# First value sums of a two-layer encoder: x transposed, cast and squared in a different order

## The chip, the cores and the metric

The kernel runs on one core of a Trainium2 chip. A core has five engines that run side by side and wait for each other through semaphores: TensorE (PE, matrix products, into PSUM), VectorE (DVE), ScalarE (ACT), GpSimd (POOL) and SyncE (SP, which here only issues DMA transfers). Each engine works through its instructions in the order in which they were issued. The metric is the device time of one execution in microseconds (us), lower is better.

## The reference

The reference is an encoder of two layers over 256 tokens of 1024 values, in float32. Each layer has a token mixer (RMSNorm, one wide input projection `w_in`, a pooling mixer, dilated attention, gates, an output projection) and a gated MLP with a short convolution. Only the very beginning of layer 0 matters here:

```python
def _rmsnorm(x, g):
    xf = x.astype(jnp.float32)
    y = xf * lax.rsqrt(jnp.mean(xf * xf, axis=-1, keepdims=True) + EPS)
    return (y * g.astype(jnp.float32)).astype(x.dtype)
...
u, q, k, v, g_pool, g_attn = jnp.split(xn @ w_in, SPLITS, axis=-1)   # xn = _rmsnorm(x, norm1)
```

## The kernel before

**Products in two parts.** TensorE multiplies in a rounded format (float32r). To keep float32's precision, every operand is split into a rounded part and a rest: h = round(a), l = a - h. A product of two such operands is three products: h*h, l*h, h*l. ScalarE makes the rounded parts ("casts") and VectorE the rests. For weights the parts are the tiles `wh` and `wl`; for x they are `xuh` and `xul`.

**Weights.** The class `Weights` (line 95) holds the list of all weight loads and of the pieces into which each load is cut. A load is 1 MB, issued by SP into one of three buffers `raw`; the next load into a buffer is issued once VectorE has made the last rest of the old one. A piece is cast into one of five pairs of buffers `wh`, `wl` (`BUFS = 5`); the buffers of piece n come free for piece n + 5 when TensorE has done its last product with piece n. The first four pieces (loads 0 and 1) and load 2 lie in tiles of their own that are needed for something else later. In layer 0, the first twelve pieces (two chunks of 128 rows by 512 columns each) belong to the values v, four to each of three groups: pieces 0 to 3 to group 0, 4 to 7 (loads 2 and 3) to group 1, 8 to 11 (loads 4 and 5) to group 2. These are multiplied by the norm's gain on the way (lines 195 to 206), one chunk of 128 x 512 per instruction. Piece 12 is the first one of the pooling projection and is cast as a whole, 128 x 1024 (line 191).

**The start of layer 0.** The mean square of x is not known when the first products could start. So `begin_values_of_x` (line 600) multiplies x as it is by the scaled weights of group 0, and the row factor (`rs`, 1 over the root of the mean square) is put on the sums afterwards (`keep_values`, line 769). x comes in four transfers: two token halves (t = 0, 1) by two halves of the 1024 values. TensorE turns x chunk by chunk of 128 values (`turn_x`, line 613, 16 transposes `xt_ps` in all), ScalarE casts the turned chunks to `xuh`, VectorE makes the rests `xul`. `square` (line 626) gives the sum of squares of one half of the values of one token half: on ScalarE for the first half of the values (line 630), on VectorE for the second (line 634); GpSimd adds them up and takes the power (lines 639 to 642). `whole` (line 644) adds `xuh` and `xul` back to a float32 x in turned form, four chunks at once (128 x 1024), for the normed x that the other projections need. `both(k)` is the cast and the rest of weight chunk k, `products` issues the products of (token half, chunk, kinds). All this is inside a hand-written order (line 785): each engine gets these instructions exactly as they are written.

**What follows.** `first_values` (line 724) transposes the two row factors (`r_ps`, line 732), scales the float32 x by gain and row factor on VectorE (line 736, eight instructions), casts it (`x2`, line 741, ScalarE, four) and takes the rests (line 742, VectorE, four). In between it keeps the sums of group 0 and computes groups 1 and 2 with 96 products on TensorE (line 754): group 1 needs pieces 4 to 7, group 2 pieces 8 to 11. Then come the parameters (`load_params`, line 355: small loads, two transposes at line 364) and the pooling projections (`proj`, line 497, products at line 492), which use `x2` and piece 12 onward. From `first_values` on, the order on each engine is not written by hand: a scheduler orders the instructions by its own estimates of when each could run. The rest of both layers is a long stream of such projections.

**Names used below.** A chunk is 128 rows of weights, or 128 values of x. A weight's rest is `wl`, and a row such as "L200 DVE wl" makes one.

Of the kernel before, what the change touches and what calls it, by code (L numbers as in the profile page):

```python
# [10 lines left out]
F32 = mybir.dt.float32  # L11
F32R = mybir.dt.float32r
AF = mybir.ActivationFunctionType
ALU = mybir.AluOpType
AX = mybir.AxisListType

P = 128
D = 1024
S = 256
DEPTH = 2  # L20
KD = D // P
# [199 lines left out]
def encoder(ctx, tc, x, w_in, w_pool, pool_scale, w_a, w_b, w_o, norm1, norm2, w_up, conv_w,  # L221
            conv_b, w_down, rel_bias, norm_f, onehot, edges, out):
    nc = tc.nc
# [5 lines left out]
    mmp = ctx.enter_context(tc.tile_pool(name="mmp", bufs=4, space=bass.MemoryType.PSUM))  # L229
# [21 lines left out]
    for l in range(DEPTH):  # L251
        for g in range(NG):
            c0 = C_V + g * 512
            slots = (("m2", 0, 2), ("m2", 1, 2), ("ybig",), ("at2",)) if g == 0 else ()
            for j in range(2):
                tag = "k1" if l == 0 and g == 1 and j == 0 else None
# [44 lines left out]
    h = const.tile([P, 2, D], F32, name="h")  # L301
# [7 lines left out]
    ident = const.tile([P, P], F32, name="ident")  # L309
# [4 lines left out]
    def begin():  # L314


        rows8 = sm.tile([KD, P], F32, tag="gain", bufs=1, name="grows")
        nc.scalar.dma_start(out=rows8, in_=norm1[0].rearrange("(k p) -> k p", p=P))
        first, second = W.load_by(4), W.load_by(2)

        def part_of_x(t, n):
            nc.sync.dma_start(out=h[:, t, HALVES[n]], in_=xv[:, t, HALVES[n]])

        part_of_x(0, 0)
        next(first)
        part_of_x(1, 0)
        for _ in range(3):
            next(first)
        part_of_x(0, 1)
        part_of_x(1, 1)  # L330
        for _ in range(2):
            next(second)
        W.load(4)
        ones = sm.tile([P, P], F32, tag="s", name="ones")
        nc.vector.memset(ones, 1.0)
        make_identity(nc, ident)
        nc.vector.memset(mhalf, -0.5)
        ps = mmp.tile([P, P], F32, tag="mm", name="gain_ps")
        warm(ps, ones, WARM[0])
        nc.tensor.transpose(ps[:, 0:KD], rows8, ident[:KD, :KD])  # L340
        nc.vector.tensor_copy(gcol, ps[:, 0:KD])
        ps = mmp.tile([P, P], F32, tag="mm", name="warm_ps")
        warm(ps, ones, WARM[1])
        return lambda n: warm(ps, ones, n)
# [255 lines left out]
    def begin_values_of_x():  # L600


        more = begin()
        W.gains = gcol

        raw_x = [
            big.tile([P, KD, 2, P], F32R, tag=tag, name=name) for tag, name in (("xn", "xuh"), ("q1", "xul"))
        ]
        xuh, xul = raw_x
        ss = [sm.tile([P, 4], F32, tag="ss", name="ss") for _ in range(2)]  # L610
        rs = [sm.tile([P, 1], F32, tag="rstd", name="rstd") for _ in range(2)]

        def turn_x(t, c0, n=4):

            ks = slice(c0, c0 + n)
            pt = mmp.tile([P, n, P], F32, tag="mm", name="xt_ps")
            for k in range(n):
                nc.tensor.transpose(pt[:, k, :], h[:, t, (c0 + k) * P : (c0 + k + 1) * P], ident)  # L618

            def keep():  # L620
                nc.scalar.copy(out=xuh[:, ks, t, :], in_=pt)
                nc.vector.tensor_sub(out=xul[:, ks, t, :], in0=pt, in1=xuh[:, ks, t, :].bitcast(F32))

            return keep

        def square(t, n):
            cc = HALVES[n]
            junk = sm.tile([P, 512], F32, tag="p", bufs=3, name="junk")
            if n == 0:
                nc.scalar.activation(  # L630
                    junk, h[:, t, cc], AF.Square, scale=D**-0.5, accum_out=ss[t][:, n : n + 1]
                )
            else:
                nc.vector.scalar_tensor_tensor(
                    out=junk, in0=h[:, t, cc], scalar=1.0 / D, in1=h[:, t, cc],
                    op0=ALU.mult, op1=ALU.mult, accum_out=ss[t][:, n : n + 1],
                )
            if n == 0:
                nc.gpsimd.tensor_scalar_add(ss[t][:, 3:4], ss[t][:, 0:1], EPS)
            else:  # L640
                nc.gpsimd.tensor_add(out=ss[t][:, 3:4], in0=ss[t][:, 3:4], in1=ss[t][:, 1:2])
                return nc.gpsimd.tensor_tensor(out=rs[t], in0=ss[t][:, 3:4], in1=mhalf, op=ALU.pow)

        def whole(n, tag):

            ks = slice(4 * n, 4 * n + 4)
            f = big.tile([P, 4, 2, P], F32, tag=tag, name="xu")
            nc.vector.tensor_add(out=f, in0=xuh[:, ks].bitcast(F32), in1=xul[:, ks].bitcast(F32))
            return f

        ps = [v_tile() for _ in range(2)]
        chunks, pieces = {}, []

        def split(k):
            if k % 2 == 0:
                pieces.append(W.n_split)
                chunks[k], chunks[k + 1] = W.open_next()
            return chunks[k]

        def product(t, k, kind):  # L660
            wh, wl = W.split[pieces[k // 2]]
            a, w = {"hh": (xuh, wh), "lh": (xul, wh), "hl": (xuh, wl)}[kind]
            first = k == 0 and kind == "hh"
            last = k == KD - 1 and kind == ("lh" if t else "hl")
            return nc.tensor.matmul(ps[t], a[:, k, t, :], w[:, k % 2, :], start=first, stop=last)  # L665

        def both(k):

            hi, lo, _ = split(k)
            hi()  # L670
            return lo()

        def products(*steps):
            for t, k, kinds in steps:
                for kind in kinds:
                    last = product(t, k, kind)
            return last

        keep = turn_x(0, 0, 2), turn_x(0, 2, 2)
        more(WARM[2])  # L680
        _, lo, hi = split(0)
        hi()
        keep[0]()
        products((0, 0, ("hh",)))
        keep = keep[1], turn_x(1, 0)
        lo()
        products((0, 0, ("lh", "hl")))
        keep[0]()
        keep[1]()
        both(1)  # L690
        products((1, 0, ("hh", "hl", "lh")))
        products(*((t, 1, (kind,)) for kind in ("hh", "lh", "hl") for t in range(2)))
        both(2)
        products(*((t, 2, ("hh", "lh", "hl")) for t in range(2)))
        keep = turn_x(0, 4)
        both(3)
        square(0, 0)
        square(1, 0)
        square(0, 1)
        f0 = whole(0, "q0")  # L700
        keep()
        products((0, 3, ("hh", "lh", "hl")))
        keep = turn_x(1, 4)
        both(4)
        keep()
        W.load(5)
        products((1, 3, ("hh", "lh", "hl")), (0, 4, ("hh", "lh", "hl")))
        both(5)
        pool = square(1, 1)
        products((1, 4, ("hh", "lh", "hl")), (0, 5, ("hh", "lh", "hl")))  # L710
        for k in range(6, KD):
            both(k)
            products((1, k - 1, ("hh", "lh", "hl")), (0, k, ("hh", "lh", "hl")))
        f1 = whole(1, "k0")
        pe = products((1, KD - 1, ("hh", "hl", "lh")))
        W.load(6)
        W.n_got = W.n_split
        for _ in range(4):
            for hi, lo, *_ in W.open_next():
                act, dve = hi(), lo()  # L720
        W.queue_behind((act, dve, pool), 4)
        return rs, raw_x, (f0, f1), ps, pe

    def first_values(rs, raw_x, fs, done, pe, keep_values):

# [36 lines left out]
    for l in range(DEPTH):  # L762
# [25 lines left out]
        else:  # L788
            for g in range(NG):
                held = begun[0] if g == 0 else [W.get() for _ in range(4)]  # L790
                for t in range(2):
                    if g + t == 0:
                        ps = begun[1]
                    else:
                        ps = v_tile()
# [18 lines left out]
        for gi in range(3, -1, -1):  # L814
# [10 lines left out]
            cur, n = u, S + 2 * PAD  # L825
            sh = 1
            while sh < w:
# [3 lines left out]
                    out=nxt[:, :, 0:n], in0=cur[:, :, 0:n], in1=cur[:, :, sh : sh + n]  # L831
# [7 lines left out]
            if hw > 1:  # L839
# [5 lines left out]
                out=pd, in0=cur[:, :, o : o + S], scalar=1.0 / w, in1=u[:, :, PAD : PAD + S],  # L845
                op0=ALU.mult, op1=ALU.subtract,
            )
            both = pl2[gi // 2][:, gi % 2 * 2 : gi % 2 * 2 + 2]
# [115 lines left out]
        for m, c in enumerate(PAIRS):  # L964
# [7 lines left out]
            for n in range(4):  # L972
# [4 lines left out]
                scale = HD**-0.5 if n < 2 else 1.0  # L977
                if hd < HPG:
# [3 lines left out]
                        out=lo[:, hd], in0=src, scalar=scale, in1=hi[:, hd].bitcast(F32),  # L982
                        op0=ALU.mult, op1=ALU.subtract,
                    )
                    nc.vector.scalar_tensor_tensor(
                        out=lo[:, hd], in0=rest, scalar=scale, in1=lo[:, hd].bitcast(F32),
                        op0=ALU.mult, op1=ALU.add,
                    )
                else:
# [3 lines left out]
                        out=o, in0=src, scalar=scale, in1=o, op0=ALU.mult, op1=ALU.add  # L993
# [20 lines left out]
        for c in range(KD):  # L1014
            th = gate(c)
            nc.vector.scalar_tensor_tensor(
                out=pa[:, c, :], in0=th, scalar=1.0, in1=pa[:, c, :], op0=ALU.add, op1=ALU.mult
# [3 lines left out]
        for c4 in range(2):  # L1021
            ths = [gate(4 * c4 + j) for j in range(4)]
            for j2 in range(2):
                i, (wh, wl) = W.get()
                for j in range(2):
                    c = 4 * c4 + 2 * j2 + j
                    ps = mmp.tile([P, 2, S], F32, tag="mm", name="b_ps")
                    cc = slice(j * P, (j + 1) * P)
# [4 lines left out]
                        out=m, in0=ths[2 * j2 + j], scalar=1.0, in1=m, op0=ALU.add, op1=ALU.mult  # L1033
# [49 lines left out]
        held, ps = entry  # L1083
        first = keep_entry(ps)
        ps = v_tile()
# [106 lines left out]
```

## Time and profile before

| what | value |
|---|---|
| median of 3 runs | 876.4 us (876.33 to 876.72) |
| the profiled execution's own time | 876.65 us |
| its span, first to last instruction | 874.9 us |
| TensorE busy | 867.3 us, 99% of the span |
| VectorE busy | 683.2 us, 78% |
| ScalarE busy | 523.2 us, 60% |
| GpSimd busy | 32.3 us, 4% |
| mean granted TensorE clock | 0.997 |
| read from memory | 159.8 MB, 184 GB/s over the span |

"Busy" is the time in which an engine had an instruction in work. TensorE's products overlap, so a row of it is longer than the distance to the next row. In a timeline a row gives the start and the length in us, the engine, the line, the operation, what it writes and reads, the shape, and how many equal instructions are put together; in brackets stands how long the engine had been idle before and what it waited for. Line numbers of the profile are those of the kernel before; in the changed kernel, lines behind the edited functions are higher by 5 or 6.

### The profile page before, as it was taken

To read this page: it belongs to the slowest core of one execution; us is meant where nothing else is said; L and a number is where in the kernel's file an instruction comes from. 1 tells how busy PE (TensorE), PEld (TensorE's weight loads), DVE (VectorE), ACT (ScalarE), POOL (GpSimd) and SP (SyncE) were. 2 spreads that over 40 slices of the span, in tenths; PEclk is the share of its full clock that TensorE was granted. 3 is DMA by queue.
4 is the path that set the end of the run, shared out by engine and by line. 5 is a ranking of instruction groups with operands and counts; after the bars stand their busy time and mean duration, and the time that the engine had idled before them with its cause. 6 is when DMAs were issued, how large, how long until landed. Compare 5 with 4: busy or idle time off the path is not lost.

```text
span 874.9 us, 12732 instructions
## 1 busy us (share of the span) xinstructions
PE 867.3 (99%) x4803; PEld 756.2 (86%) x4803; DVE 683.2 (78%) x1160; ACT 523.2 (60%) x927; POOL 32.3 (4%) x98
## 2 busy tenths in 40 slices
PE   9999999999999999999999999999999999999997
PEld 7888898988888888888888888898888888888886
DVE  7998786767869988878756988676678698877874
ACT  6756554556747766666545564554666486656662
POOL 2700000000000000000000000000000000000000
PEclk9999999999999999999999999999999999999998
DMA  9675645355555465465737465543556447456441
GB/s 331 228 250 198 199 153 171 124 172 190 177 186 194 163 226 189 167 219 191 241 121 240 145 215 171 163 161 121 186 189 216 152 150 254 164 193 210 175 145 49
DMA packets 125958, 161.70 MB, mean 185 GB/s; under 512 B 3320, under 2 KB 106432, under 8 KB 125896
## 3 DMA queue, kind: packets, MB, share of 16 engines
q1 hardware_dynamic: 125880, 160.88, 54.5%
q8 instruction: 38, 0.62, 0.3%
q14 instruction: 24, 0.20, 0.1%
q10 hardware_dynamic: 16, 0.00, 0.0%
HBM read 159.80 MB, written 1.07 MB: 184 GB/s over the span
## 4 chain that ended last, share of the span: by engine, by line
PE 99%; ACT 0%; POOLq 0%; DVE 0%; issue 0%; POOL 0%; ACTq 0%
PE proj_ps L492 61%; PE v_ps L590 6%; PE res_ps L520 6%; PE res_ps L522 6%; PE res_ps L521 6%; PE b_ps L492 3%; PE v_ps L754 2%; PE v_ps L665 1%; PE pool_ps L492 1%; PE o_ps L945 1%; PE s_ps L895 1%; PE pt_ps L924 1%; PE s_ps L890 1%; PE o_ps L941 1%; PE xt_ps L458 1%; PE xt_ps L618 0%
## 5 line engine op out<-in xcount | busy, mean ns | idle before, releaser
L192 DVE TENSOR_TENSOR wl<-raw,wh 128x1024 fp32r<-128x1024 f32 x274 | 333.9, 1223 | 85.1 <-ACT wh L191 83.3
L492 PE MATMUL proj_ps<-x,wh 128*128 128x512 f32 x1408 | 343.7, 392 | 0.0
L191 ACT CAST wh<-raw 128x1024 fp32r<-128x1024 f32 x274 | 286.8, 1050 | 78.9 <-PE res_ps L522 39.0
L492 PEld LDWEIGHTS proj_ps<-x,wh 128*128 128x128 f32 x1408 | 257.7, 188 | 49.3
L492 PEld LDWEIGHTS proj_ps<-x,wl 128*128 128x128 f32 x1408 | 180.8, 191 | 6.9
L492 PE MATMUL proj_ps<-x,wl 128*128 128x256 f32 x1408 | 183.7, 283 | 0.0
L520 PE MATMUL res_ps<-wh,actq 128*128 128x512 f32 (+1 forms) x184 | 70.0, 380 | 0.0
L521 PE MATMUL res_ps<-wl,actq 128*128 128x512 f32 (+1 forms) x184 | 69.9, 380 | 0.0
L522 PE MATMUL res_ps<-wh,actk 128*128 128x512 f32 (+1 forms) x184 | 69.9, 380 | 0.0
L1105 ACT ACTIVATE y<-a,prm 128x256 f32<-128x256 f32 x36 | 21.6, 601 | 40.5 <-DVE a L516 40.5
L521 PEld LDWEIGHTS res_ps<-wl,actq 128*128 128x128 f32 x184 | 34.6, 188 | 6.6
L520 PEld LDWEIGHTS res_ps<-wh,actq 128*128 128x128 f32 x184 | 34.6, 188 | 6.6
L522 PEld LDWEIGHTS res_ps<-wh,actk 128*128 128x128 f32 x184 | 34.6, 188 | 6.6
L492 PE MATMUL proj_ps<-po,wh 128*128 128x512 f32 x128 | 32.2, 396 | 0.0
L431 POOL TENSOR_SCALAR ss<-ss 128x1 f32<-128x1 f32 x8 | 2.1, 266 | 800.3 <-ACT junk L424 800.3
L1106 DVE SCALAR_TENSOR_TENSOR y<-a,prm,y 128x255 f32<-128x255 f32 x36 | 17.3, 482 | 14.1 <-ACT y L1105 14.1
L492 PEld LDWEIGHTS proj_ps<-po,wh 128*128 128x128 f32 x128 | 23.1, 189 | 4.2
L424 ACT ACTIVATE junk<-h 128x512 f32<-128x512 f32 (+1 forms) x20 | 11.0, 548 | 26.4 <-DVE h L422 26.4
L520 PE MATMUL res_ps<-wh,m 128*128 128x512 f32 (+1 forms) x72 | 26.5, 368 | 0.0
L522 PE MATMUL res_ps<-wh,m 128*128 128x512 f32 (+1 forms) x72 | 26.3, 366 | 0.0
L521 PE MATMUL res_ps<-wl,m 128*128 128x512 f32 (+1 forms) x72 | 26.3, 365 | 0.0
L590 PE MATMUL v_ps<-wh,x 128*128 128x512 f32 x80 | 25.7, 392 | 0.0
(202 smaller groups left out, 1125.5 us busy)
## 6 DMA issues: line engine op xcount, KB each, us to landing
raw<-in_w_in_dram SPq DMA_DIRECT2D x58, 1024.0 KB, 5.9
raw<-in_w_up_dram SPq DMA_DIRECT2D x44, 1024.0 KB, 5.1
raw<-in_w_down_dram SPq DMA_DIRECT2D x22, 1024.0 KB, 4.9
raw<-in_w_a_dram SPq DMA_DIRECT2D x8, 1024.0 KB, 5.0
raw<-in_w_o_dram SPq DMA_DIRECT2D x8, 1024.0 KB, 4.9
raw<-in_w_b_dram SPq DMA_DIRECT2D x4, 1024.0 KB, 4.8
raw<-in_w_pool_dram SPq DMA_DIRECT2D x2, 1024.0 KB, 5.1
gain<-in_norm_dram SPq DMA_DIRECT2D x3, 512.0 KB, 4.6
```

Source lines behind the costliest of these rows:

```text
L191: lambda: nc.scalar.copy(out=h, in_=src),
L192: lambda: nc.vector.tensor_sub(out=l, in0=src, in1=h.bitcast(F32)),
L424: nc.scalar.activation(junk[:, 0 : cc.stop - cc.start], h[:, t, cc], AF.Square, scale=D**-0.5, accum_out=ss[:, n : n + 1],)
L458: nc.tensor.transpose(pt[:, k, :], xn[:, c0 : c0 + P], ident)
L492: nc.tensor.matmul(out, w(k), x, start=(n == 0), stop=(n == 2 * nk - 1), skip_group_check=turns["rest"])
L520: nc.tensor.matmul(ps, ah, wh, start=first, stop=False)
L521: nc.tensor.matmul(ps, ah, wl, start=False, stop=False)
L522: nc.tensor.matmul(ps, al, wh, start=False, stop=last)
L590: nc.tensor.matmul(ps, x2[:, 2 * n + j, part, t, :], w[:, j, :], start=(n + m == 0), stop=(n == 3 and m == 5),)
L754: nc.tensor.matmul(ps[t], a[:, k, t, :], w[:, j, :], start=(k + m == 0), stop=(k == KD - 1 and m == 2),)
L1105: nc.scalar.activation(y, a, AF.Identity, bias=b, scale=w1)
L1106: nc.vector.scalar_tensor_tensor(out=y[:, 1:], in0=a[:, : S - 1], scalar=w0, in1=y[:, 1:], op0=ALU.mult, op1=ALU.add)
```

## The change

Nothing is computed differently; the transfers and the number of transposes, casts of weights and products stay as they are. In `begin_values_of_x`:

- `turn_x` takes a list of token halves. At the start it turns, casts and rests chunks 0 and 1 of token half 0, then chunks 0 and 1 of token half 1, then chunks 2 and 3 of both token halves in one piece. Before, these were chunks 0 and 1 and chunks 2 and 3 of token half 0, and all four chunks of token half 1. Chunks 4 to 7 stay in two pieces, one for each token half; the first of them now stands among the products of chunk 2 instead of behind them.
- All four squares are done by ScalarE, and they are spread: one ahead of the cast of weight chunk 4, one ahead of chunk 5, one ahead of chunk 6, one behind chunk 7.
- The two sums `whole` are made behind the rests of pieces 5 and 7 of the weights, instead of among the rests of x and behind the rest of weight chunk 7.
- The products of chunks 0 to 2 are interleaved in another order.

```diff
--- before.py
+++ after.py
@@ -610,31 +610,32 @@
         ss = [sm.tile([P, 4], F32, tag="ss", name="ss") for _ in range(2)]
         rs = [sm.tile([P, 1], F32, tag="rstd", name="rstd") for _ in range(2)]
 
-        def turn_x(t, c0, n=4):
+        def turn_x(ts, c0, n):
+
 
             ks = slice(c0, c0 + n)
-            pt = mmp.tile([P, n, P], F32, tag="mm", name="xt_ps")
-            for k in range(n):
-                nc.tensor.transpose(pt[:, k, :], h[:, t, (c0 + k) * P : (c0 + k + 1) * P], ident)
+            pt = mmp.tile([P, n, len(ts), P], F32, tag="mm", name="xt_ps")
+            for j, t in enumerate(ts):
+                for k in range(n):
+                    nc.tensor.transpose(
+                        pt[:, k, j, :], h[:, t, (c0 + k) * P : (c0 + k + 1) * P], ident
+                    )
+            tt = slice(ts[0], ts[-1] + 1)
 
             def keep():
-                nc.scalar.copy(out=xuh[:, ks, t, :], in_=pt)
-                nc.vector.tensor_sub(out=xul[:, ks, t, :], in0=pt, in1=xuh[:, ks, t, :].bitcast(F32))
+                nc.scalar.copy(out=xuh[:, ks, tt, :], in_=pt)
+                nc.vector.tensor_sub(
+                    out=xul[:, ks, tt, :], in0=pt, in1=xuh[:, ks, tt, :].bitcast(F32)
+                )
 
             return keep
 
         def square(t, n):
             cc = HALVES[n]
             junk = sm.tile([P, 512], F32, tag="p", bufs=3, name="junk")
-            if n == 0:
-                nc.scalar.activation(
-                    junk, h[:, t, cc], AF.Square, scale=D**-0.5, accum_out=ss[t][:, n : n + 1]
-                )
-            else:
-                nc.vector.scalar_tensor_tensor(
-                    out=junk, in0=h[:, t, cc], scalar=1.0 / D, in1=h[:, t, cc],
-                    op0=ALU.mult, op1=ALU.mult, accum_out=ss[t][:, n : n + 1],
-                )
+            nc.scalar.activation(
+                junk, h[:, t, cc], AF.Square, scale=D**-0.5, accum_out=ss[t][:, n : n + 1]
+            )
             if n == 0:
                 nc.gpsimd.tensor_scalar_add(ss[t][:, 3:4], ss[t][:, 0:1], EPS)
             else:
@@ -676,50 +677,55 @@
                     last = product(t, k, kind)
             return last
 
-        keep = turn_x(0, 0, 2), turn_x(0, 2, 2)
+        every = ("hh", "lh", "hl")
+        keep = turn_x((0,), 0, 2)
         more(WARM[2])
         _, lo, hi = split(0)
         hi()
-        keep[0]()
+        keep()
         products((0, 0, ("hh",)))
-        keep = keep[1], turn_x(1, 0)
+        keep = turn_x((1,), 0, 2)
         lo()
-        products((0, 0, ("lh", "hl")))
-        keep[0]()
-        keep[1]()
+        products((0, 0, ("lh",)))
+        keep()
+        keep = turn_x((0, 1), 2, 2)
         both(1)
-        products((1, 0, ("hh", "hl", "lh")))
-        products(*((t, 1, (kind,)) for kind in ("hh", "lh", "hl") for t in range(2)))
+        products((0, 0, ("hl",)), (1, 0, ("hh", "hl", "lh")))
+        keep()
         both(2)
-        products(*((t, 2, ("hh", "lh", "hl")) for t in range(2)))
-        keep = turn_x(0, 4)
+        products((0, 1, ("hh", "lh")), (1, 1, ("hh", "lh")), (0, 1, ("hl",)), (1, 1, ("hl",)))
         both(3)
+        products((0, 2, ("hh", "lh")), (1, 2, ("hh", "lh")))
+        keep = turn_x((0,), 4, 4)
+        products((0, 2, ("hl",)), (1, 2, ("hl",)))
+        keep()
         square(0, 0)
-        square(1, 0)
-        square(0, 1)
-        f0 = whole(0, "q0")
-        keep()
-        products((0, 3, ("hh", "lh", "hl")))
-        keep = turn_x(1, 4)
+        products((0, 3, every))
+        keep = turn_x((1,), 4, 4)
         both(4)
         keep()
         W.load(5)
-        products((1, 3, ("hh", "lh", "hl")), (0, 4, ("hh", "lh", "hl")))
+        products((1, 3, every), (0, 4, every))
+        square(1, 0)
         both(5)
+        products((1, 4, every), (0, 5, every))
+        square(0, 1)
+        both(6)
+        products((1, 5, every), (0, 6, every))
+        both(7)
         pool = square(1, 1)
-        products((1, 4, ("hh", "lh", "hl")), (0, 5, ("hh", "lh", "hl")))
-        for k in range(6, KD):
-            both(k)
-            products((1, k - 1, ("hh", "lh", "hl")), (0, k, ("hh", "lh", "hl")))
-        f1 = whole(1, "k0")
+        products((1, 6, every), (0, 7, every))
         pe = products((1, KD - 1, ("hh", "hl", "lh")))
         W.load(6)
         W.n_got = W.n_split
-        for _ in range(4):
+        fs = []
+        for n in range(4):
             for hi, lo, *_ in W.open_next():
                 act, dve = hi(), lo()
+            if n % 2:
+                fs.append(whole(n // 2, ("q0", "k0")[n // 2]))
         W.queue_behind((act, dve, pool), 4)
-        return rs, raw_x, (f0, f1), ps, pe
+        return rs, raw_x, fs, ps, pe
 
     def first_values(rs, raw_x, fs, done, pe, keep_values):
```

The scheduler's order of what follows changes with it, up to about the second product of the pooling projections. On ScalarE the casts of `x2` stand further back: before, two of the four are ahead of the first cast of piece 9, and now all four are behind it. On TensorE the two transposes of the parameters and the first two products of the pooling projection (with piece 12) are now among the products of group 2: the transposes behind its first product, the pair behind the first product with piece 9. On SP the load of pieces 10 and 11 is issued behind one more of the small parameter loads. Everything later is in the same order as before.

## The prediction

> **What bounds the kernel now.** I read the page first, then the chain of waits, then the timelines of TensorE, ScalarE and VectorE, engine by engine, over the first 46 us, which is all that the change touches: set side by side, the two programs issue the same instructions in the same order on every engine from about 46 us on.
>
> ```profile
> span 874.9 us, 12732 instructions
> PE 867.3 (99%) x4803; PEld 756.2 (86%) x4803; DVE 683.2 (78%) x1160; ACT 523.2 (60%) x927; POOL 32.3 (4%) x98
> PE 99%; ACT 0%; POOLq 0%; DVE 0%; issue 0%; POOL 0%; ACTq 0%
> ```
>
> TensorE is busy for 99% of the span and is 99% of the chain. A change in the first 46 us therefore costs what it adds to TensorE's waits there, and gains what it takes from them; the dense stream behind passes it on to the end. The TensorE rows of the start (start, length, engine, line, operation, out<-in, form, count, idle time before):
>
> ```profile
> 4.26 1.06 PE L618 MATMUL xt_ps<-ident,h 128*128 128x128 f32 x4
> 7.08 0.40 PE L665 MATMUL v_ps<-m,xuh 128*128 128x512 f32 x1
> 7.69 0.74 PE L665 MATMUL v_ps<-m,xuh 128*128 128x512 f32 x2 [0.21 <-ACT xuh L621]
> 8.41 0.50 PE L665 MATMUL v_ps<-m,xul 128*128 128x512 f32 x1
> 11.51 0.60 PE L618 MATMUL xt_ps<-ident,h 128*128 128x128 f32 x4
> 14.25 0.68 PE L665 MATMUL v_ps<-ybig,xuh 128*128 128x512 f32 x2
> 14.80 0.50 PE L665 MATMUL v_ps<-ybig,xul 128*128 128x512 f32 x1
> 19.47 0.38 PE L732 MATMUL r_ps<-ident,rstd 128*128 128x128 f32 x2
> 30.58 0.39 PE L754 MATMUL v_ps<-wh,xuh 128*128 128x512 f32 x1
> ```
>
> In a dense stretch a 512-column product starts 0.227 us after the last one (its row, 0.39 long, holds 0.165 of drain), a transpose 0.109. From 7.08 to 19.47 lie 46 products and 8 transposes, 11.3 us dense, in 12.4: 1.05 us are waits (0.37 before 7.69, 0.16 before 8.41, under 0.1 before 14.25 and 14.80, and each time some 0.11 until the stream runs again). Behind 19.47 there is none: the 96 products of L754 follow each other without a gap up to 41.5. ScalarE, start and second stage:
>
> ```profile
> 8.91 1.37 ACT L199 ACTIVATE m<-raw,gcol 128x512 fp32r<-128x512 f32 x2 [0.66 <-DMA raw<-in_w_in_dram]
> 10.19 0.62 ACT L630 ACTIVATE junk<-h 128x512 f32<-128x512 f32 x1
> 10.71 0.19 ACT L630 ACTIVATION_READ_ACCUMULATOR junk<-h 128x1 f32 x1
> 26.76 1.34 ACT L199 ACTIVATE wh<-raw,gcol 128x512 fp32r<-128x512 f32 x2 [0.22 <-PE v_ps L754]
> 28.00 0.60 ACT L741 CAST x<-xu 128x512 fp32r<-128x512 f32 x1
> 28.51 0.72 ACT L199 ACTIVATE wh<-raw,gcol 128x512 fp32r<-128x512 f32 x1
> 29.14 0.60 ACT L741 CAST x<-xu 128x512 fp32r<-128x512 f32 x1
> 29.64 1.95 ACT L199 ACTIVATE wh<-raw,gcol 128x512 fp32r<-128x512 f32 x3
> 31.50 1.04 ACT L191 CAST wh<-raw 128x1024 fp32r<-128x1024 f32 x1
> ```
>
> Chunk 2 of the first weights starts at 8.91, when it lands. From 26.76 on ScalarE has no idle time up to the wide cast of piece 12, and 26.76 itself is TensorE giving back the buffer of piece 4. VectorE:
>
> ```profile
> 17.26 1.22 DVE L648 TENSOR_TENSOR xu<-xuh,xul 128x1024 f32<-128x1024 f32 x1
> 18.39 5.38 DVE L200 SCALAR_TENSOR_TENSOR wl<-raw,gcol,wh 128x512 fp32r<-128x512 f32 x8
> 29.26 0.74 DVE L200 SCALAR_TENSOR_TENSOR wl<-raw,gcol,wh 128x512 fp32r<-128x512 f32 x1
> 30.52 0.74 DVE L200 SCALAR_TENSOR_TENSOR wl<-raw,gcol,wh 128x512 fp32r<-128x512 f32 x1
> ```
>
> The two rests of piece 8 are ready at 30.00 and 31.26; TensorE wants them at 30.81 and 31.49, so VectorE is only 0.8 and 0.2 us ahead.
>
> **The change, part by part.** Pitches (start to next start) from these rows and their neighbours: scaled cast 0.62 to 0.64, square with its readout 0.62, cast of x to two parts (L741) 0.51, cast of 512 values of x 0.48, weight rest 0.66, sum of x's parts 1.14, scaling (L736) 0.39, subtraction (L742) 0.61. A result is seen by another engine some 0.05 later.
>
> *Up to the first sums.* Transposes, casts and rests come in smaller pieces, so the wait before 7.69 goes: token half 1 is cast at 6.4 instead of 7.05, chunk 1's cast follows when it lands, near 7.08 instead of 7.53, and TensorE gets through chunks 0 and 1 by 9.5. What is late next is chunk 2: landed at 8.91, cast at 9.64, first product at 9.70, a wait of 0.2 plus 0.11. From there 36 products and 8 transposes remain, 36 x 0.227 + 8 x 0.109 = 9.05, which would end at 18.86. But ScalarE now does all four squares (2 x 0.62 more), each between two casts: x's second half is cast at 11.36 (its transposes now stand behind four products of chunk 2), square to 12.46, chunk 4's cast ready at 13.19, its rest at 13.97, wanted at 13.87; the rest of x's token half 1 and chunk 5's rest come 0.05 and 0.1 late in the same way. With 0.11 each that is 0.6: 19.5 against 19.47. I take nothing. The ends: with no late rest 18.86, a gain of 0.6; with every late rest twice as late and the next square in front of it, a loss of 0.5. VectorE's two squares (0.68 each) are gone, but it only waits for ScalarE instead. GpSimd's sums (0.6 and 0.95 after a square) follow the last square, now near 16.7 to 17.4, and are done at 19.1 against 19.5 wanted: 0.4 of cover, each tenth beyond it would cost a tenth.
>
> *The sums of x's parts behind pieces 5 and 7.* ScalarE reaches piece 4 at 17.34 instead of 16.02, VectorE starts its rests at 18.1 instead of 18.39. Four rests and the first sum: 18.1 + 4 x 0.66 + 1.14 = 21.9, piece 6's first rest ready at 22.64, wanted at 22.9: 0.26 of cover, and no cost. Four more rests and the second sum: VectorE is free at 25.7, where it was at 23.69: two microseconds later in a stretch in which it was 0.2 to 0.8 us ahead.
>
> *What the order does with it.* The part of the program behind the hand-written order is put in order by a scheduler, and there three things move. ScalarE now has the first half of piece 9 ahead of all four casts of x to parts (L741), which before had two of them done by then; that half still waits for TensorE to give back piece 4's buffer, at 26.76. TensorE has two products of the first pooling projection (L492, piece 12) and the two parameter transposes (L364) moved forward among the L754 products; the pair stands behind the first product of piece 9. Nothing behind the pair can start before the wide cast of piece 12. On ScalarE that cast now has six scaled casts and four casts of x in front, counted from 26.76: 6 x 0.62 + 4 x 0.51 + 1.04 = 6.80, ready at 33.56, seen at 33.6. (The same sum with two casts of x gives 32.54 for before, which is what the row says: 31.50 + 1.04.) TensorE would come to the pair 7 products and two transposes (0.17, L364) after 30.58, at 32.34. It waits 1.26, and 0.11 to run again: 1.37. The release at 26.76 is itself a TensorE time, so an earlier or later start moves both.
>
> VectorE's lateness shows at the same place. Five scalings to 27.7, the first cast of x ready at 28.0 behind piece 9, two subtractions, three scalings: piece 8's first rest is ready at 31.2 (wanted 30.98), the second, behind another subtraction, at 32.45 (wanted about 32.0). These waits lie ahead of the pair and inside its wait; alone, if ScalarE were in time, they would cost 0.2 + 0.45 + 0.22 = 0.87. The rests of pieces 9 to 11, 1.8 us later than before, meet a TensorE that is 1.4 later plus 0.45 of moved products: 0.5 of cover, as before.
>
> *Queues.* On SP the load of piece 10's weights goes behind one small parameter load and waits for load 3's landing (18.55) instead of load 2's: issued near 18.6, not 17.36. Loads in front of it are still landing at 21.46, and its cast is due near 29; at the 5.9 us that such loads take it lands by 24.5. The next loads are given free by VectorE 1.8 us later, some 6 us ahead of use. Nothing is taken for either; if a load were late, up to 1.3.
>
> *Sum.* 0.0 + 1.37 on a profiled execution of 876.65 (span 874.9, 1.75 around it): 878.0. That execution is 0.25 above the median of 876.4; against the median, **877.8**.
>
> **Rivals.** *Waits that add up* (slower by more than 0.2%, which is 1.75 us and about what a measurement of this kernel can tell from no change): the start loses its 0.5 because the squares stand ahead of casts that TensorE wants, or rests of pieces 6 and 7 use up their 0.26; either moves the release of piece 4's buffer and the pair's wait comes on top. 876.4 + 1.37 + 0.4 to 0.9: 878.2 to 878.7, taken at 878.4. For it: ScalarE is busy without a break from 11.4 on. Against: half of the sum's small waits are under a tenth.
>
> *A late clock* (slower): four transposes take 1.06 at 4.26 and 0.60 at 11.51, pitches of 0.213 and 0.109, and the first product at the full pace is that of 7.08. So TensorE runs at half pace until about 6.9, some 5.8 us after its first instruction at 1.04. The changed order leaves it idle for 0.2 near 5.1, where it had none: two transposes and one idle multiplication are over before x is cast. If that gap starts the count anew, full pace comes at 11.1: 4.2 us at half pace lose 2.1, of which the wait for chunk 2 hides 0.3, so 1.8 on top of 1.37: 879.6. Against: before had gaps of 0.2 and more at 7.5 and the pace stayed. The Trainium skill (TensorE: Matmul & The Clock Gate, Part 1, the HAM clock gate) says that the array runs at half rate until a free-running window of some 3.4 us has been busy, and drops back only after an idle window. By that rule a spoilt window would cost one window more, an estimate of 1.3 instead of 1.8, and a gap of 0.2 would most likely spoil none; the trace agrees in the two paces.
>
> *The start gains* (slower by less): no late rest, TensorE at 19.47 0.6 earlier, the pair's wait unchanged since its start moves too, up to the 0.26 of cover on piece 6's rests: 876.4 + 1.37 - 0.3 to 0.6, 877.2.
>
> *The pair does not wait* (not slower): ScalarE is in time for piece 12, so only the start counts: 876.4 - 0.6 to 876.4, say 876.0. It needs 1.26 off the 6.80 of ScalarE's queue, which the rows of before do not give, or VectorE's waits ahead of the pair to vanish as well; otherwise their 0.87 stays.
>
> **How the numbers follow.** Forecast, 876.9 to 878.1 around 877.8: 0.46. Waits that add up, 878.4: 0.33. Late clock, 879.6: 0.07. The start gains, 877.2: 0.08. The pair does not wait, 876.0: 0.06. Range 876.7 to 879.0: it leaves out the late clock and the last case, 0.13. Slower by over 0.2% (above 878.15) is the second case, the late clock and a tail of 0.03 of the forecast: 0.43; faster (below 874.65) needs the last case and over a microsecond more, 0.02; the rest, 0.55, within.
>
> **What would show it.** In the changed kernel's timeline: the wait of 0.21 at 7.69 gone and one of 0.2 near 9.7 in its place; r_ps near 19.5; L648 among the weight rests near 20.8 and 24.6; TensorE idle before wl of piece 8 (0.2 to 0.5, released by VectorE) and before proj_ps near 33.6 (released by ScalarE, L191); everything behind 46 us later by 1.4. If r_ps comes before 19.0 or after 19.9, the start was mis-sized; if the pair starts without a wait near 32.4, the main term is wrong.

## The result, and the profile after

The changed kernel takes 879.0 us (median of 7 runs, 878.16 to 879.83), the kernel before beside it 876.4 us (876.03 to 876.72): 1.0027 times as long, with a 95% interval of 1.0017 to 1.0037. It is slower, by 0.27% or some 2.4 to 2.6 us, where the prediction had 1.4. The profiled execution takes 879.0 us, 2.35 more than that of before (876.65). Its page says of the whole:

```profile
span 877.1 us, 12735 instructions
PE 869.3 (99%) x4803; PEld 757.0 (86%) x4803; DVE 682.3 (78%) x1156; ACT 524.2 (60%) x931; POOL 30.1 (3%) x98
```

TensorE is still busy for 99% of a span that is 2.3 us longer. The instructions are as foretold: two squares, of two instructions each, less on VectorE (1156 for 1160) and more on ScalarE (931 for 927). In the changed file the lines behind the start are shifted: transposes are L620, casts of x L626, rests of x L627, squares L636, products of the start L666, sums of x's parts L649, r_ps L738, group 2's products L760, their casts and rests of x L747 and L748, and values' rests L785.

Two points split the span: the first r_ps, which ends the start, and the first product with wl of the pooling projection, which ends the stage of group 2. All the rest lasts 831.4 in every kernel of this study.

| | r_ps at | from there to the pooling projection | rest | span |
|---|---|---|---|---|
| before | 19.47 | 24.05 | 831.35 | 874.87 |
| changed | 20.39 | 25.38 | 831.36 | 877.13 |
| difference | +0.92 | +1.33 | 0.0 | +2.26 |

The stage behind r_ps has grown by nearly what the prediction's main term said, 1.37. The start, which was to cost nothing, has grown by 0.9. First the stage, in TensorE's timeline of the changed kernel (start, length, engine, line, operation, out<-in, form, count, idle time before and who ended it):

```profile
31.74 0.33 PE L364 MATMUL prm_ps<-ident,prow 96*128 96x96 f32 x2
32.08 0.50 PE L760 MATMUL v_ps<-wl,xuh 128*128 128x512 f32 x1
...
32.66 0.40 PE L760 MATMUL v_ps<-wh,xuh 128*128 128x512 f32 x1
33.34 0.51 PE L760 MATMUL v_ps<-wl,xuh 128*128 128x512 f32 x1 [0.29 <-DVE wl L200]
...
33.92 0.40 PE L760 MATMUL v_ps<-wh,xuh 128*128 128x512 f32 x1
34.49 0.74 PE L492 MATMUL proj_ps<-x,wh 128*128 128x512 f32 x2 [0.17 <-ACT wh L191]
35.07 0.40 PE L760 MATMUL v_ps<-wh,xuh 128*128 128x512 f32 x1
```

The idle time in brackets counts only what is left when a row's drain is over, so the loss is read from the starts. Between 31.74 and 32.08 lie 0.34, where the two transposes at their pitch of 0.085 need 0.17: 0.17 for the first rest of piece 8. Between 32.66 and 33.34 lie 0.68 where 0.23 would do: 0.45 for the second rest of piece 8. Between 33.92 and 34.49 lie 0.57: 0.34 for the wide cast of piece 12. Each time the next start comes 0.11 late as well, which makes 1.29 of the 1.33. The same stage on ScalarE and on VectorE:

```profile
27.62 0.73 ACT L199 ACTIVATE wh<-raw,gcol 128x512 fp32r<-128x512 f32 x1 [0.44 <-PE v_ps L760]
...
33.40 1.03 ACT L191 CAST wh<-raw 128x1024 fp32r<-128x1024 f32 x1
```

```profile
21.55 1.22 DVE L649 TENSOR_TENSOR xu<-xuh,xul 128x1024 f32<-128x1024 f32 x1
22.69 2.74 DVE L200 SCALAR_TENSOR_TENSOR wl<-raw,gcol,wh 128x512 fp32r<-128x512 f32 x4
25.34 1.22 DVE L649 TENSOR_TENSOR xu<-xuh,xul 128x1024 f32<-128x1024 f32 x1
...
31.28 0.75 DVE L200 SCALAR_TENSOR_TENSOR wl<-raw,gcol,wh 128x512 fp32r<-128x512 f32 x1
...
32.54 0.75 DVE L200 SCALAR_TENSOR_TENSOR wl<-raw,gcol,wh 128x512 fp32r<-128x512 f32 x1
...
33.80 1.41 DVE L785 SCALAR_TENSOR_TENSOR vl<-v_ps,rstd,vh 128x512 fp32r<-128x512 f32 x2
```

From TensorE's release at 27.62 to the end of the wide cast at 34.43 ScalarE has no break: 6.81, against the 6.80 that were worked out. The sums stand behind four weight rests each, at 21.55 and 25.34, later than foretold by no more than r_ps is. Now the start on TensorE:

```profile
4.69 0.63 PE L349 MATMUL warm_ps<-ones 128*128 128x128 f32 x2
5.36 0.80 PE L666 MATMUL v_ps<-m,xuh 128*128 128x512 f32 x1
...
8.94 0.57 PE L666 MATMUL v_ps<-m,xul 128*128 128x512 f32 x1
9.35 0.39 PE L666 MATMUL v_ps<-m,xuh 128*128 128x512 f32 x1
...
20.39 0.38 PE L738 MATMUL r_ps<-ident,rstd 128*128 128x128 f32 x2
```

A product of 512 columns has a row of 0.6 to 0.8 at half pace and of 0.39 at full pace. The change between them, which the granted clock in the trace puts at 9.32, came at 6.87 in the kernel before. TensorE has nothing to do from 5.12 (4.69 and two pitches of 0.213) to 5.36: this is the gap near 5.1 that the prediction's late clock spoke of. The wait before 7.69 is gone, but it is gone inside a stretch at half pace.

### The profile page after: what moved, and what is told of

It is laid out like the page before. It is cut to its first block, busy times and chain, and to the rows that moved or that the text cites. A ratio compares the mean times of both kernels' runs of the same rounds, so it can differ in the third digit from the quotient of the medians.

```text
span 877.1 us, 12735 instructions
## 1 busy us (share of the span) xinstructions
PE 869.3 (99%) x4803; PEld 757.0 (86%) x4803; DVE 682.3 (78%) x1156; ACT 524.2 (60%) x931; POOL 30.1 (3%) x98
## 4 chain that ended last, share of the span: by engine, by line
PE 95%; ACT 0%; POOLq 0%; DVE 0%; issue 0%; POOL 0%; ACTq 0%
PE proj_ps L492 61%; PE v_ps L590 6%; PE res_ps L522 6%; PE res_ps L521 6%; PE res_ps L520 6%; PE b_ps L492 3%; PE pool_ps L492 1%; PE v_ps L760 1%; PE o_ps L951 1%; PE s_ps L901 1%; PE pt_ps L930 1%; PE s_ps L896 1%; PE o_ps L947 1%; PE xt_ps L458 1%; PE a_turn L1085 0%; ACT xn L475 0%
## 5 line engine op out<-in xcount | busy, mean ns | idle before, releaser
L1112 DVE SCALAR_TENSOR_TENSOR y<-a,prm,y 128x255 f32<-128x255 f32 x36 | 17.5, 485 | 14.1 <-ACT y L1111 14.1
```

What stands on the lines that cost most here:

```text
L1112: nc.vector.scalar_tensor_tensor(out=y[:, 1:], in0=a[:, : S - 1], scalar=w0, in1=y[:, 1:], op0=ALU.mult, op1=ALU.add)
```

## The experiments

Two questions were open. Is the stage's loss due to the two moved sums, and what in it holds TensorE? And is the start late through the gap near 5.1 (below called theory gap), through a pace that comes when it likes (theory phase), or through the squares on ScalarE (theory S)? The experiments ran on three chips, each with the kernel before beside them: its median was 876.13 us beside the first four experiments, 876.21 beside the next four and 876.63 beside the last. Each ratio is against these executions; it is not the quotient of the two medians.

**The sums, put back.** The changed kernel, with both sums where they were:

```diff
+        f0 = whole(0, "q0")
         products((0, 3, every))
...
+        f1 = whole(1, "k0")
         pe = products((1, KD - 1, ("hh", "hl", "lh")))
...
-        fs = []
+        fs = [f0, f1]
...
-            if n % 2:
-                fs.append(whole(n // 2, ("q0", "k0")[n // 2]))
```

> The changed kernel with the two sums of x's parts back where they stood before. Theory P (of the +2.6 us some 1.4 are the pair's wait, which the moved sums cause through the scheduler's order, and the rest is the clock: TensorE reaches its full pace at a time that differs from one execution to the next, and the new start is exposed to it where the old one waited anyway): in this program the pair is back behind the products of group 2 and two casts of x are ahead of piece 9, so the pair's wait is gone; 876.5 to 877.8 us, median near 877.3, with r_ps near 19.5 when full pace comes at 6.9 and near 20.4 when it comes at 9.3. Theory S (the four squares on ScalarE make everything behind late, and the sums matter little): 878.5 us or more.

Measured: 877.1 us (876.13 to 879.1), ratio 1.0008 (0.9998 to 1.0018). From r_ps to the pooling projection 24.07, as before (24.05): the stage's loss is gone, with all its waits. r_ps, however, comes at 21.04, later still; full pace came at 10.07, and the first sum now stands ahead of a rest that TensorE wants:

```profile
15.77 0.73 PE L666 MATMUL v_ps<-ybig,xuh 128*128 128x512 f32 x2 [0.43 <-DVE ybig L200]
...
21.04 0.38 PE L738 MATMUL r_ps<-ident,rstd 128*128 128x128 f32 x2
```

**The sums alone.** The kernel before, with only the two sums moved as in the change:

```diff
-        f0 = whole(0, "q0")
...
-        f1 = whole(1, "k0")
...
-        for _ in range(4):
+        fs = []
+        for n in range(4):
             for hi, lo, *_ in W.open_next():
                 act, dve = hi(), lo()
+            if n % 2:
+                fs.append(whole(n // 2, ("q0", "k0")[n // 2]))
```

> The kernel before with nothing changed but the two sums of x's parts, which are made behind the rests of pieces 5 and 7. In this program's order one product of the pooling projection stands ahead of group 2's end. Theory P: the wait on ScalarE's wide cast appears, 0.9 to 1.4 us on 876.4, so 877.3 to 877.8, r_ps still near 19.5. Theory S: 876.4 to 876.8, since the squares are not moved.

Measured: 877.47 us (876.76 to 879.2), ratio 1.001 (1.0001 to 1.0019). The stage takes 24.90, 0.85 more than before, and the start 19.01. TensorE's timeline:

```profile
30.35 0.33 PE L364 MATMUL prm_ps<-ident,prow 96*128 96x96 f32 x2
30.73 0.50 PE L755 MATMUL v_ps<-wl,xuh 128*128 128x512 f32 x1
...
31.30 0.39 PE L755 MATMUL v_ps<-wh,xuh 128*128 128x512 f32 x1
31.99 0.50 PE L755 MATMUL v_ps<-wl,xuh 128*128 128x512 f32 x1 [0.30 <-DVE wl L200]
...
32.79 0.40 PE L492 MATMUL proj_ps<-x,wh 128*128 128x512 f32 x1
```

Only the two rests of piece 8 hold TensorE here: 0.2 ahead of 30.73 and 0.46 ahead of 31.99, each with 0.11 behind it, which is the stage's 0.85. The time is the one expected, but not by the expected wait on the wide cast. The scheduler brings one product of piece 12 forward, not two, and it doesn't wait. So the sums alone make the greater part of the loss, through VectorE; the wait for the wide cast is the rest of it, and it needs the other changes of the order.

**The pair, held back.** The changed kernel, with the first two products of the pooling projection not to be issued before the last product of group 2:

```diff
+                            W.last_v = nc.tensor.matmul(
...
+                with ExitStack() as held:
+                    if l == 0 and (gi, j) == (3, 0):
+                        held.enter_context(tc.issue_after(W.last_v.ins))
+                    sums = proj(x2)
-                add_up(in_order(u[:, j, PAD : PAD + S]), [halves(a) for a in proj(x2)])
+                add_up(in_order(u[:, j, PAD : PAD + S]), [halves(a) for a in sums])
```

> The changed kernel with the first products of the pooling projection held on TensorE behind the last product of group 2; nothing else is moved. The pair then can't wait for piece 12's cast. If the pair's place alone were the cost, 1.4 us less than the changed kernel, 877.6. If VectorE's late rests of piece 8 take over, as the prediction has it (0.87 of its 1.37 stays), 0.5 less: 878.5.

Measured: 879.25 us (877.67 to 879.55, 6 runs), ratio 1.0027 (1.0015 to 1.0038). That is above both of the expected figures, with full pace at 9.59. The stage takes 25.47, no less than the changed kernel's 25.38. TensorE, and VectorE at the same time:

```profile
33.51 0.50 PE L760 MATMUL v_ps<-wl,xuh 128*128 128x512 f32 x1 [0.30 <-DVE wl L200]
...
34.08 0.40 PE L760 MATMUL v_ps<-wh,xuh 128*128 128x512 f32 x1
34.77 0.50 PE L760 MATMUL v_ps<-wh,xuh 128*128 128x512 f32 x1 [0.30 <-DVE vl L785]
```

```profile
33.98 1.40 DVE L785 SCALAR_TENSOR_TENSOR vl<-v_ps,rstd,vh 128x512 fp32r<-128x512 f32 x2
```

The pair is out of the way, and the next product now waits 0.46 (0.69 from start to start, less 0.23) for VectorE, which has to read the sums of the other token half out of their buffer (L785) before TensorE may write there. In the changed kernel that wait lay inside the pair's. So keeping the pair out of the way saves nothing in this stage, and the wide cast is not the price by itself. What costs 1.3 is VectorE being two sums late; where the order shows it is secondary.

**The gap, filled.** The changed kernel with one idle multiplication more behind the first two transposes:

```diff
-WARM = (5, 1, 1)
+WARM = (5, 1, 2)
```

> The changed kernel with one more idle multiplication ahead of the first product, so that TensorE has no gap between the first transposes and the first product. Theory gap (the 0.2 us of idle time near 5.1 puts off the full pace): full pace near 6.9 again, r_ps near 19.6, 877.8 to 878.0 us. Theory phase (the moment of full pace comes from a clock that doesn't follow the kernel; the gap has no part in it): as the changed kernel, 878.2 to 879.8, median near 879.0, and the moment differs from run to run.

Measured: 877.9 us (877.14 to 878.5), ratio 1.0013 (1.0004 to 1.0022). The stage is that of the changed kernel, 25.33, but r_ps comes at 18.65: full pace came at 5.27. TensorE has no gap, and is at full pace with its first product. The median is the one that theory gap had named; the pace came earlier than its 6.9:

```profile
4.69 0.89 PE L349 MATMUL warm_ps<-ones 128*128 128x128 f32 x4
5.45 0.47 PE L666 MATMUL v_ps<-m,xuh 128*128 128x512 f32 x1
...
6.57 0.95 PE L666 MATMUL v_ps<-m,xuh 128*128 128x512 f32 x3
```

**The gap, alone.** The kernel before without its idle multiplication at 5.11, so that TensorE is idle from 5.11 to 5.40:

```diff
-WARM = (5, 1, 1)
+WARM = (5, 1, 0)
```

> The kernel before without the idle multiplication ahead of its first product, and so with the same gap of 0.2 us near 5.1 that the changed kernel has. In the six profiles so far full pace came at 6.9, 6.0 and 5.3 in kernels without the gap and at 9.3, 9.6 and 10.1 in kernels with it. Theory gap: here it comes near 8.5 to 11.3 as well (or ahead of 5.1, in a fifth of the executions); the old order hides some of it behind its wait at 7.7, so 876.1 to 877.3, median near 876.7, 0.5 above the kernel before of the same job, and r_ps at 19.5 to 20.6. Theory phase (the gap has no part in it): as the kernel before, median within 0.2 of it.

Measured: 876.64 us (875.88 to 877.68), ratio 1.0002 (0.9993 to 1.0011), so by the time not to be told from before. By the profile full pace came at 8.98 instead of 6.87 and r_ps at 19.77 instead of 19.47:

```profile
5.40 0.76 PE L665 MATMUL v_ps<-m,xuh 128*128 128x512 f32 x1
...
7.24 1.67 PE L665 MATMUL v_ps<-m,xuh 128*128 128x512 f32 x3
8.71 0.52 PE L665 MATMUL v_ps<-m,xul 128*128 128x512 f32 x1
9.07 0.63 PE L665 MATMUL v_ps<-m,xuh 128*128 128x512 f32 x2
```

At half pace the old order's wait at 7.69 doesn't occur, its price being paid in pace instead; so the old order has little to lose by a late pace.

**The changed kernel once more**, for other executions of the same program:

> The changed kernel once more, beside the others on one chip. Theory gap: 878.2 to 879.8, median near 879.0, full pace between 8.5 and 11.3 in the profile; r_ps to the pooling projection's rests 25.4. Theory phase: the moment of full pace can lie anywhere between 4.5 and 7.9 as well, and the median is near 878.2 in another set of executions.

Measured: 878.13 us (877.21 to 879.74), ratio 1.002 (1.0011 to 1.0029), and the same stage, 25.38. In its profile full pace came at 10.11, and TensorE waited 0.76 for a late transfer of x besides (1.19 from the start of the product before, at 5.48, less its 0.43), which no other profile shows:

```profile
6.67 0.69 PE L620 MATMUL xt_ps<-ident,h 128*128 128x128 f32 x2 [0.42 <-DMA h<-in_x_dram]
```

So the late pace is what theory gap expected, and the median of 878.1 is what theory phase named.

**The squares, alone.** The kernel before, with all squares by ScalarE:

```diff
-            if n == 0:
...
-            else:
-                nc.vector.scalar_tensor_tensor(
...
+            nc.scalar.activation(
+                junk, h[:, t, cc], AF.Square, scale=D**-0.5, accum_out=ss[t][:, n : n + 1]
+            )
```

> The kernel before with all four squares on ScalarE at the places where they are issued now, nothing else. The prediction took nothing for this: 876.1 us, as the kernel before of the same job to within 0.2. Theory S (ScalarE's extra 1.24 us come late for TensorE): 0.5 or more above.

Measured: 876.64 us (876.08 to 877.18), ratio 1.0003 (0.9994 to 1.0011): 0.4 by the medians, not to be told from none. The profiled execution, with full pace at 4.87, has r_ps at 18.83 and a stage of 24.10.

**Small pieces without the two losses.** The sums back as in the first experiment and the gap filled:

> The changed kernel with both causes taken away: the sums of x's parts where they were before, and one more idle multiplication that fills the gap. Theory gap and theory P together: full pace between 4.5 and 7.9, r_ps 18.6 to 19.6, from r_ps to the pooling projection's rests 24.05 as before; 875.3 to 876.3 us, median near 875.9, 0.2 below the kernel before. Theory phase: as the variant with the sums back, 877.1.

Measured: 876.5 us (876.06 to 877.21), ratio 1.0003 (0.9994 to 1.0012). By the medians that is 0.3 above the kernel before, where 0.2 below was expected. Stage 24.11, r_ps 19.53 with full pace at 6.76, as good as before's 19.47 with 6.87. The first sum stands here on VectorE between chunk 3's and chunk 4's work, and the rest behind it (13.46) holds TensorE for 0.6:

```profile
12.33 1.22 DVE L649 TENSOR_TENSOR xu<-xuh,xul 128x1024 f32<-128x1024 f32 x1
13.46 0.75 DVE L200 SCALAR_TENSOR_TENSOR ybig<-raw,gcol,ybig 128x512 fp32r<-128x512 f32 x1
```

**And that sum earlier.** The same with the first sum moved up to behind chunk 3's weights, out of that rest's way:

```diff
         both(3)
+        f0 = whole(0, "q0")
         products((0, 2, ("hh", "lh")), (1, 2, ("hh", "lh")))
```

> The changed start with the gap filled, the four squares on ScalarE, and the first sum of x's parts moved into VectorE's idle time behind chunk 3's rest (some 2 us there), the second where it was before. The variant with the sums back waited 0.6 + 0.11 + 0.11 for chunk 4's rest, which stood behind the first sum. If that is all that keeps the new start from paying: r_ps at 18.8 when full pace comes at 6.8 (19.53 there), stage behind it 24.05 to 24.1; median 0.3 to 0.6 us below the kernel before of the same job, 875.6 to 875.9. If the squares on ScalarE are late by themselves (late by 0.1 and 0.11 twice, as in the changed kernel): no better than before, 876.1 to 876.4.

Measured: 876.42 us (875.88 to 879.0), ratio 1.0001 (0.9992 to 1.0009). The wait of 0.6 is gone, five small ones of 0.08 to 0.11 between 14.1 and 16.2 stay, r_ps is at 19.59 with full pace at 7.40, the stage 24.11. Of the two expectations the second, that of squares which are late by themselves, is the nearer. No version here is shown to be faster than the kernel before.

**What the profiles say together.**

| kernel | gap near 5.1 | full pace at | r_ps | stage |
|---|---|---|---|---|
| squares alone | no | 4.87 | 18.83 | 24.10 |
| changed, gap filled | no | 5.27 | 18.65 | 25.33 |
| sums alone | no | 5.96 | 19.01 | 24.90 |
| sums back, gap filled | no | 6.76 | 19.53 | 24.11 |
| before | no | 6.87 | 19.47 | 24.05 |
| the same, first sum earlier | no | 7.40 | 19.59 | 24.11 |
| before, with gap | yes | 8.98 | 19.77 | 24.11 |
| changed | yes | 9.32 | 20.39 | 25.38 |
| pair held back | yes | 9.59 | 20.55 | 25.47 |
| sums back | yes | 10.07 | 21.04 | 24.07 |
| changed, again | yes | 10.11 | 21.21 | 25.38 |

Six of six without the gap lie below 7.5, five of five with it above 8.9. (The squares' kernel is idle there too, for 0.27, but behind its full pace.) So both theories on the clock hold a part in these profiles: the pace comes at a moment that differs between executions by some 2.5 us, and with the gap it comes later.

The traces' own record of the granted clock shows how the two go together. Full pace lasts 863.572 us in seven profiles and 866.985 us in the other four, which is 253 and 254 times 3.4133: the clock changes on a grid of 3.41 us. Count one such step back from each full pace. In the five profiles with the gap the step before holds the gap (2.50 to 5.91 in the changed kernel), and the step that ends in full pace begins behind it. In the six without, the step before begins ahead of TensorE's first instruction at 1.04 and holds the idle time up to there. How much idle time a step can bear is not settled: a hole of 0.14 at 3.33, which every kernel has, lies in three steps that did end in full pace (squares alone, gap filled, sums alone), while the gaps of 0.24 to 0.36, which come on top of that hole, put it off.

What the times show is weaker. Three orders were run with the gap and without it: the changed one (ratios 1.002 and 1.0027 with, 1.0013 without), that with the sums back (1.0008 and 1.0003) and that of before (1.0002 and 1). With the gap it is slower each time, by 0.2 to 1.2 us, but the intervals overlap each time, and the medians of the changed order, 878.13 with the gap and 877.9 without, are nearly one. Nor, to judge by the times, does the gap delay every execution: the shortest of the changed kernel, 877.21 us, is nearly as short as the profiled one with the gap filled, 877.14.

## Why the prediction was right in its main term and wrong in another

The number came out well in part by luck. 879.0 is the very end of the range of 876.7 to 879.0, which was closed there to leave out the late clock, and it lies above the forecast's own band of 876.9 to 878.1. The same program had 878.1 in a second set of executions.

*The pair's wait, +1.37.* It came as +1.33, +1.33 and, with the gap filled, +1.28; putting the sums back takes all of it away. ScalarE's queue was right to 0.01. The waits show where they were foretold: 0.17 and 0.45 for VectorE's two rests (foretold 0.2 and 0.45) and 0.34 for the pair, each with its 0.11.

*"Alone, if ScalarE were in time, VectorE's waits would cost 0.87".* With the sums alone, where the pair doesn't wait, it is 0.85. But holding the pair back in the changed order didn't bring the stage down to that: 1.42. The sum had left out the rests of the values (L785), which VectorE also does late, and which give TensorE its buffers back. The pair's wait hid that one: the first of these rests starts at 33.80 and is 0.75 long, so it ends 0.1 behind the wide cast's 34.43. Two limits that end together gave the number of one.

*The start, "I take nothing".* This is the term that failed: it measured +0.9 in the profile, and r_ps after 19.9 was the prediction's own sign of it. At one pace its sum holds, by an estimate only. The two profiles of the changed order, with and without the gap, have r_ps at 20.39 and 18.65 with full pace at 9.32 and 5.27: each microsecond by which the pace is later costs 1.74 / 4.05 = 0.43. At the 6.87 of before, the changed order would reach r_ps at 20.39 - 2.45 x 0.43 = 19.34, an estimate that lies 0.13 from before's 19.47. The wait of 0.2 foretold near 9.7 for chunk 2 doesn't appear: its cast starts at 8.38, right behind the work in front of it, where in the execution of before it had to wait until 8.91 for its transfer; with the gap filled it starts earlier still. The small late rests do appear: five losses of 0.07 to 0.11 between 14.9 and 17.0, restarts among them. That ScalarE would be busy without a break from 11.4 didn't hold, as it waits 2.54 us for TensorE up to 12.26. The five losses add up to 0.5 and are there with the gap filled too; the prediction had 0.6 for them. Theory S is left with at most the 0.4 of the squares' experiment.

*The late clock, given 0.07.* This is what the two profiles of the changed kernel show; the times were 879.0 and 878.1 instead of 879.6. What failed is the sentence against it, "before had gaps of 0.2 and more at 7.5 and the pace stayed". Those gaps lay behind the change of pace. They say that a short gap doesn't end full pace, and nothing on whether one delays it. The two are different questions, and before had no gap of 0.2 in its stretch at half pace to answer the second. The Trainium skill (TensorE: Matmul & The Clock Gate, Part 1, the HAM clock gate) has a free-running window of some 3.4 us that must be busy. The traces agree with that in four ways: the clock changes on a grid of 3.41 us, the moment of full pace differs between executions, the band without the gap (2.5 us) is narrower than one window, and with the gap the band begins some 4 us later. An estimate from that rule: TensorE starts at 1.04, so the first busy window ends between 1.04 + 3.4 = 4.4 and 7.9 (seen: 4.87 to 7.40); a window that begins behind the gap, at 5.4, ends at 8.8 or later (seen: 8.98 to 10.11). The prediction had read the same rule as saying that 0.2 of 3.4 us "would most likely spoil none"; in the profiles it does, with the limit that the times set to this.

*Waits that add up, 0.33.* Some 0.9 on top of the pair's wait is what the profile has, but by another cause: with the gap filled r_ps comes at 18.65, with the same squares on ScalarE and the same rests.

*The queues, nothing.* Neither TensorE, VectorE nor ScalarE waits for a load of weights in the changed stage. The rest of the program, 831.4 in both, shows that the later loads had their cover.

*The start gains, 877.2, and the pair doesn't wait, 876.0.* With the gap filled the start does come earlier (18.65), by pace and not by fewer waits. A start at 19.01 in the sums' experiment didn't shorten the stage behind it.

## What to carry to other kernels

Moving work "behind the next weights" on an engine with a few tenths of a microsecond of cover costs what exceeds that cover, wherever the order lets it surface: if the visible wait is taken away, look for the next result that the same late engine owes. Work at a kernel's start is to be checked for holes in TensorE's stream, not only for its sum; a hole of 0.2 us that no wait hides can cost a microsecond in an execution, by the estimate of 0.43 for each microsecond of delay, if it comes before full pace; here one more idle multiplication filled it, for a gain in the times that is not clear of their spread. Evidence that a gap is harmless holds only for the phase in which that gap was seen.

## What the runs showed of the hardware

- A gap of 0.24 to 0.36 us in TensorE's stream near 5.1 us, before full pace, goes with full pace at 8.98 to 10.11 us instead of 4.87 to 7.40 (five profiles with it, six without). By the times it does not delay every execution.
- Full pace lasts 253 or 254 times 3.4133 us in every profile (863.572 or 866.985 us), so the clock changes on a grid whose place differs between executions.
- The moment of full pace differs by 2.5 us between the profiles without a gap, though TensorE's rows are the same up to 4.26, and r_ps goes with it: 18.65 to 19.59 over the different orders. One program, run twice, had it at 9.32 and 10.11. Part of the spread of 1 to 2 us between the times of one kernel may come from that; this was not measured apart.
- After a wait of TensorE the second start comes 0.11 late as well: in the changed kernel 33.69 and 32.42 follow 33.34 and 32.08 by 0.34 to 0.35, where 0.23 is the pitch. A cause was not looked for.
